# Four PSUM banks as single tiles and two as pairs, another order of the row pairs, and a 64-byte shift of the large SBUF pools

## The chip, the cores and the metric

The kernel runs on one NeuronCore of one Trainium2 chip. The metric is the device time of one execution in microseconds, as a median over runs. The engines named below are PE (TensorE, matmuls), PEld (its weight loads), DVE (VectorE), ACT (ScalarE), POOL (GpSimd) and SP (the queue from which weight loads are issued).

## The reference

A two-layer trunk on 256 tokens of width 2048, in float32. Each layer is a token mixer and then an MLP, with an RMS norm ahead of each and one at the end.

```
x (1, 256, 2048); D_FF = 8192
layer 0: x += conv_module(rms_norm(x))   # pw1 + GLU, causal depthwise conv of 31, LayerNorm, silu, pw2
         x += square(relu(rms_norm(x) @ mlp_w1[0])) @ mlp_w2[0]
layer 1: x += mla(rms_norm(x))           # w_in, low-rank q and kv, rotary key, 16 heads, softmax, w_o
         x += square(relu(rms_norm(x) @ mlp_w1[1])) @ mlp_w2[1]
out = rms_norm(x)
```

The four MLP products are the bulk: each is 256 x 2048 x 8192 or 256 x 8192 x 2048.

## The kernel before

**Split products.** A float32 operand is held as two parts, hi (rounded to the TensorE's fp32r) and lo (the rest). A product is three matmuls, hi·hi, lo·hi and hi·lo (`mm3`, L215 to L217). Weights come from DRAM as `raw` tiles by SP; ACT makes `hi` (L182 or L509), DVE makes `lo` (L186 or L510). Three `raw` tiles and six each of `hi` and `lo` are in turn. In `mm3` the activation (a 128x128 slice of a tile such as `gh`, `sh`, `fh`, `xh`, `xt`) is the operand that stands in the array and the weight tile, 512 columns wide, moves through it. In the plain up blocks (L796, L797) the weights stand and the activations, `xt`, move.

**The MLP.** It runs in two halves of 4096 hidden columns. The up product of a half has six steps in the order of `UP_PLAN`: four plain blocks of 512 columns each, and two up blocks (`up_block`), with two blocks of 512 columns together each. An up block takes the 2048 input rows as eight row pairs of 2 x 128 rows, in the order `UP_ORDER`. Four of them (2, 3, 4 and 5, `UP_MIXED`) are mixed: seven products (21 matmuls) stand for eight, of sums and differences of the input, prepared once (`fh`, `fl`), and of the weights, prepared per pair on DVE (`mixed_weights`: L517 to L519 change `raw`, L509 and L510 split the results). The other four are plain: eight products (24 matmuls) and only two `hi` and two `lo`. There are eight up blocks in a run, two for each layer and half. The down product of a half adds mixed and plain row pairs in the same way, for two column blocks at a time; the last one of the kernel ends with two single column blocks, and the last of these with a split end that the final norm follows. Their sums are in `Sums`: four banks `e`, in which row block t and column block c have one bank each, and four banks `u` for the mixed products.

**PSUM.** There are eight banks of 512 float32 values per partition. In the MLP the pool is four tiles of two banks each (`pair`); a single bank is half of such a tile (`acc_tile`, `spare`). A tile is given out again when its users are done, tile by tile, and both halves of a pair count as one tile.

**Order.** Each engine runs its instructions in the order in which the kernel writes them; instructions wait on semaphores for their inputs and for the buffer that they write.

**SBUF.** Tiles get their addresses in the order in which the pools are opened. A pad tile of `PAD_SMALL` columns (4 bytes each) stands ahead of the pools of each stage, so it shifts all of these.

Of the kernel before, what the change touches and what calls it, by code (L numbers as in the profile page):

```python
# [37 lines left out]
PAD_SMALL = 48  # L38
# [8 lines left out]
UP_PLAN, UP_ORDER, UP_MIXED = (4, 5, 0, 6, 2, 7), (0, 2, 3, 1, 4, 5, 6, 7), (2, 3, 4, 5)  # L47
# [35 lines left out]
def trunk_kernel(  # L83
# [33 lines left out]
    psum, psum_cx, spare = {}, [ExitStack()], []  # L117

    def repool(name, **banks):

        psum_cx[0].close()
        psum_cx[0] = ExitStack()
        psum.clear()
        spare.clear()
        for kind, n in banks.items():
            psum[kind] = psum_cx[0].enter_context(tc.tile_pool(name=kind + name, bufs=n, space=PSUM, reuse_waits="tile"))
# [147 lines left out]
    def to_T(src, k0, hi, lo, gain, rest=None):  # L274
# [12 lines left out]


        def lower():
            for j in range(2):  # L290
                lo_part(ps[j], hi(k0 + j), lo(k0 + j), gain[:, k0 + j : k0 + j + 1])

        if rest is None:
            lower()
        else:
            while rest:
                rest.pop(0)()
            rest.append(lower)
# [89 lines left out]
    def residual_stage(last, gain, r_scale=None, raw=None, by_steps=()):  # L388
# [18 lines left out]
        def prepare(n, only=None, half=None, out=None, rest=None):  # L407
            sl = columns(n, half)
            if last:
                if n in by_steps:  # L410
                    step()
                    steps.extend(turn_block(n, gain, raw))
                elif gain is not None:
                    while rest:
                        rest.pop(0)()
                    for j in range(2):
                        to_T(xs, 4 * n + 2 * j, xh, xl, gain, rest if j == 1 else None)
# [11 lines left out]
    def product_A(  # L429
        w, k_lo, nk, hi, lo, add, prepare, blocks=range(NNB), due=(), finish=None, before=None,  # L430
        units=None, banks=None, begun=None, beside=None, room=None,
# [12 lines left out]
        for n in blocks:  # L444
            ps = [acc_tile() for _ in range(T)] if banks is None else banks[n]
# [28 lines left out]
            if n_end:  # L474
                before()
                for t in range(T):
# [160 lines left out]
    def mlp(layer, ssq, next_gain, finish=None, before=None, beside=None, after_up=None):  # L637

        with ExitStack() as cx:
# [5 lines left out]
            repool(f"mlp{layer}", pair=4)  # L645
# [12 lines left out]
            def spread(r):  # L658
                o = [pair_tile() for _ in range(2)][0][:, 0, :]
# [56 lines left out]
            def up_block(hf, g, fs, copies):  # L716

                n = (hf * nkh + 4 * g) // 4
                sums = Sums(n, False, False)
# [18 lines left out]
                for t, z in enumerate(zs):  # L738
                    o = z.rearrange("p (c n) -> p c n", c=2)
                    nc.vector.tensor_tensor(o, sums.pe[t], o, op=ALU.add)  # L740
                    nc.scalar.activation(z, z, AF.Relu, scale=r_cols[0][:, t : t + 1])

                def turned():
                    pts = [a.rearrange("p b (k t n) -> p (b k) t n", t=T, n=P) for a in sums.pe]
# [11 lines left out]
                for _ in range(2):  # L756
                    pair_tile()
# [3 lines left out]
            for hf in range(HALVES):  # L761
# [10 lines left out]
                for nth, g in enumerate(UP_PLAN):  # L772
# [3 lines left out]
                    pairs = [pair_tile() for _ in range(2)]  # L776
                    ps = [a[:, b, :] for a in pairs for b in range(2)]
                    if layer > 0 and hf == nth == 0:
                        nc.vector.memset(ps[3][:, 0:1], 0.0)  # L779
# [30 lines left out]
                    for i, a in enumerate(pairs):  # L810
                        vi = v[:, 2 * i : 2 * i + 2, :]
# [78 lines left out]
    with ExitStack() as cx:  # L890
# [544 lines left out]
        product_A(conv_w_pw2[0], 0, KC, sh_kt, sl_kt, add, prepare, range(2, NNB), range(2))  # L1435
# [66 lines left out]
    with ExitStack() as cx:  # L1502
# [329 lines left out]
        with tc.manual_schedule():  # L1832
# [8 lines left out]
            free = [acc_tile() for _ in range(6)]  # L1841
            ps = [free[:2], free[2:4]]

            def kv_products(k, ts):
                u, j = divmod(k, 2)
                wh, wl = w_at(("kv", u), j)
                for t in ts:
                    for i in range(2):
                        ns = slice(i * NKV, (i + 1) * NKV)
                        if k == t == 0 and i == 1:  # L1850
                            for o in free[4:]:
                                nc.vector.memset(o[:, 0:1], 0.0)
                            for o in ps[1][::-1]:
                                nc.scalar.activation(o[:, 0:1], ident[:, 0:1], AF.Copy)
# [131 lines left out]
        product_A(mla_w_o[0], 0, H, oh_kt, ol_kt, add, prepare, range(2, NNB), range(2))  # L1986
# [90 lines left out]
```

## Time and profile before

| | |
|---|---|
| median of 3 runs | 1951.13 us (1950.62 to 1952.14) |
| profiled execution: its time, and the span of its trace | 1951.48 us, 1949.6 us |
| PE busy | 1928.1 us, 99% of the span |
| DVE busy | 1694.4 us, 87% |
| ACT busy | 1192.6 us, 61% |
| DMA | 193 GB/s on average |

Share of the chain of work that ended last: PE 86%, DVE 10%, ACT 2%. A busy PE does not say that nothing is lost: the ends of matmuls are modelled, and they overlap. Where PE loses time is seen from starts: from one start of a 128x512 matmul to the next it is about 0.23 us, and a larger step is a stall. The column in brackets behind a row of the timeline gives the idle time ahead of it and the instruction that ended it.

### The profile page before, as it was taken

How to read it: one execution, taken by the hardware profiler on the slowest of the kernel's cores; microseconds unless marked ns; L12 is line 12 of the kernel's file. 1: busy time of each engine (PE TensorE's matmuls, PEld its weight loads, DVE VectorE, ACT ScalarE, POOL GpSimd, SP SyncE). 2: the span in 40 equal slices, each digit the busy share in tenths (PEclk: the TensorE clock that was granted, in tenths of full speed). 3: DMA queues.
4: the chain of work that ended last, by engine and by line, in shares of the span. 5: the costliest groups of instructions: out<-in, count | busy, mean ns of one | idle time of the engine just before them, and what ended most of it. 6: DMA issues, size and time to landing. Idle time of an engine off the chain costs nothing.

```text
span 1949.6 us, 27537 instructions
## 1 busy us (share of the span) xinstructions
PE 1928.1 (99%) x10245; PEld 1654.1 (85%) x10245; DVE 1694.4 (87%) x2382; ACT 1192.6 (61%) x1655; POOL 248.7 (13%) x208
## 2 busy tenths in 40 slices
PE   9999999999999999999999999999999999999997
PEld 9999888888888888888889998888788888878886
DVE  7999988988989898899976766898999988898896
ACT  5667756656556656655576655566665556666554
POOL 6999200000010100000002310000000010000000
PEclk9999999999999999999999999999999999999998
DMA  7766455546575854655565545545647685565763
GB/s 227 213 187 182 160 186 191 200 154 212 194 243 187 248 196 163 216 190 199 195 195 151 141 152 173 178 167 195 225 149 238 219 242 180 195 216 195 226 206 119
DMA packets 214038, 375.43 MB, mean 193 GB/s; under 512 B 16392, under 2 KB 107792, under 8 KB 213648
## 3 DMA queue, kind: packets, MB, share of 16 engines
q1 hardware_dynamic: 208256, 363.28, 56.4%
q0 software_dynamic: 4320, 7.87, 2.3%
q10 hardware_dynamic: 1328, 2.52, 0.4%
q8 instruction: 80, 1.31, 0.3%
q14 instruction: 54, 0.44, 0.1%
HBM read 363.68 MB, written 2.10 MB: 188 GB/s over the span
## 4 chain that ended last, share of the span: by engine, by line
PE 86%; DVE 10%; ACT 2%; issue 2%; DMA 0%; DVEq 0%; ACTq 0%
PE pair L215 15%; PE pair L217 15%; PE pair L216 14%; PE pair L796 10%; PE acc L955 8%; PE pair L797 6%; PE acc L215 4%; PE acc L217 4%; PE acc L216 4%; PE acc L1419 2%; DVE lo L510 2%; DVE sum L1042 1%; DVE raw L517 1%; ACT hi L509 1%; DVE sl L538 1%
## 5 line engine op out<-in xcount | busy, mean ns | idle before, releaser
L182 ACT ACTIVATE hi<-raw 128x1024 fp32r<-128x1024 f32 (+2 forms) x510 | 508.1, 1029 | 182.9 <-DMA raw<-in_mlp_w 62.4
L186 DVE TENSOR_TENSOR lo<-raw,hi 128x1024 fp32r<-128x1024 f32 (+2 forms) x445 | 518.2, 1192 | 112.0 <-ACT hi L182 105.6
L509 ACT ACTIVATE hi<-raw 128x1024 fp32r<-128x1024 f32 x376 | 347.3, 948 | 320.5 <-DVE raw L517 191.8
L510 DVE TENSOR_TENSOR lo<-raw,hi 128x1024 fp32r<-128x1024 f32 x376 | 400.5, 1087 | 33.8 <-ACT hi L509 28.6
L796 PE MATMUL pair<-xt,hi 128*128 128x512 f32 x1024 | 357.2, 391 | 0.4 <-DVE pair L779 0.2
L797 PE MATMUL pair<-xt,lo 128*128 128x256 f32 x1024 | 288.6, 282 | 0.0
L796 PEld LDWEIGHTS pair<-xt,hi 128*128 128x128 f32 x1024 | 192.2, 188 | 41.2 <-issue 0.6
L215 PE MATMUL pair<-hi,gh 128*128 128x512 f32 (+1 forms) x516 | 203.5, 394 | 3.9 <-DVE xs L400 3.9
L217 PE MATMUL pair<-lo,gh 128*128 128x512 f32 (+1 forms) x516 | 202.4, 392 | 0.0
L216 PE MATMUL pair<-hi,gl 128*128 128x512 f32 (+1 forms) x516 | 200.7, 389 | 0.0
L797 PEld LDWEIGHTS pair<-xt,lo 128*128 128x128 f32 x1024 | 193.5, 189 | 0.5
L955 PE MATMUL acc<-xt,hi 128*128 128x256 f32 x1024 | 180.1, 281 | 0.4 <-ACT xt L1222 0.3
L215 PE MATMUL pair<-hi,sh 128*128 128x512 f32 x450 | 177.1, 393 | 0.0
L217 PE MATMUL pair<-lo,sh 128*128 128x512 f32 x450 | 176.5, 392 | 0.0
L216 PE MATMUL pair<-hi,sl 128*128 128x512 f32 x450 | 174.9, 389 | 0.0
L596 POOL DMA_DIRECT2D xs<-v x30 | 26.2, 909 | 1142.4 <-ACT v L614 1082.8
L1042 DVE SCALAR_TENSOR_TENSOR sum<-ub,w_dw,sum 128x256 f32<-128x256 f32 x409 | 164.4, 485 | 3.5 <-ACT sum L1012 3.0
L186 POOL TENSOR_TENSOR lo<-raw,hi 128x1024 fp32r<-128x1024 f32 x65 | 155.1, 2412 | 17.9 <-ACT hi L182 17.9
L955 PEld LDWEIGHTS acc<-xt,hi 128*128 128x128 f32 x1024 | 154.6, 188 | 1.2 <-ACT xt L1222 0.8
L955 PE MATMUL acc<-xt,lo 128*128 128x256 f32 x512 | 139.2, 279 | 0.0
L215 PEld LDWEIGHTS pair<-hi,gh 128*128 128x128 f32 x516 | 97.6, 189 | 24.1 <-ACT hi L182 3.8
L217 PEld LDWEIGHTS pair<-lo,gh 128*128 128x128 f32 x516 | 97.5, 189 | 22.1
(354 smaller groups left out, 3555.8 us busy)
## 6 DMA issues: line engine op xcount, KB each, us to landing
raw<-in_mlp_w SPq DMA_DIRECT2D x255, 1024.0 KB, 5.4
raw<-in_conv_w_pw SPq DMA_DIRECT2D x62, 512.0 KB, 5.1
raw<-in_conv_w_pw SPq DMA_DIRECT2D x16, 1024.0 KB, 5.0
raw<-in_mla_w_o SPq DMA_DIRECT2D x16, 1024.0 KB, 5.1
raw<-in_mla_w_kv_up SPq DMA_DIRECT2D x32, 256.0 KB, 3.8
xs<-v POOLq DMA_DIRECT2D x30, 256.0 KB, 7.7
raw<-in_mla_w_in SPq DMA_DIRECT2D x8, 576.0 KB, 3.8
raw<-in_mla_w_in SPq DMA_DIRECT2D x4, 1024.0 KB
```

The source lines that it names most:

```text
L182: nc.scalar.activation(hi, raw[:, js, :], AF.Copy)
L186: eng.tensor_tensor(lo, raw, hi.bitcast(F32), op=ALU.subtract)
L215: nc.tensor.matmul(ps, sh, mh, start=start, stop=False)
L216: nc.tensor.matmul(ps, sl, mh, start=False, stop=False)
L217: nc.tensor.matmul(ps, sh, ml, start=False, stop=stop)
L509: nc.scalar.activation(hi, src, AF.Copy)
L510: nc.vector.tensor_tensor(lo, src, hi.bitcast(F32), op=ALU.subtract)
L796: nc.tensor.matmul(ps[b], wh[:, bs], xhl(k), start=k == 0, stop=False)
L797: nc.tensor.matmul(ps[b][:, :S], wl[:, bs], xh(k), start=False, stop=k == KC - 1)
L955: nc.tensor.matmul(pss[c][b][:, :S], w[i][:, bs], (xh, xl)[j](k), start=k == i + j == 0, stop=end and k == k0 + nk - 1 and (i, j) == terms ...
L1042: nc.vector.scalar_tensor_tensor(out=out, in0=ubs[c][:, w : w + S], scalar=tap(c, w), in1=base, op0=ALU.mult, op1=ALU.add)
L1419: nc.tensor.matmul(ps2[b][t], x_kt(k, t), w[:, bs], start=k == g == i == 0, stop=k == KC - 1 and i == len(group) - 1,)
```

## The change

1. `UP_ORDER` becomes (0, 2, 1, 3, 6, 4, 5, 7): a plain pair stands between mixed pairs 2 and 3, and another between 3 and 4.
2. In the MLP the PSUM pool becomes four single banks (`acc`) and two pairs (`pair`), opened in one order in layer 0 and in the other in layer 1. `Sums` takes two pairs and four singles; in the down products the banks `e` are the pairs for the first two column blocks and the singles for the others. Plain up blocks after the first use four singles, and add up their halves in four operations of 256 columns rather than two of 512. The two halves at the very end of the kernel use two different pairs.
3. At the end of layer 0's MLP the eight transposes of a column block go to one pair and are issued together (`block_T`), with the `lo` parts of the last two of its four row blocks put off; before it was two tiles of one bank with four transposes each (`to_T`).
4. At three stage ends a bank is passed over by a memset of one column (`passed`, and `free[0]` in the attention stage), and two memsets and copies that did so before are left out.
5. `PAD_SMALL` goes from 48 to 64 columns: all pools behind it move by 64 bytes. For the large pools, whose tiles stand in the array, the offset of a tile goes from 64 to 0 modulo 128 bytes; `hi`, `lo`, `raw` (0), `xt` (32) and the pools on the right side stay where they were.

```
-PAD_SMALL = 48
+PAD_SMALL = 64
-UP_PLAN, UP_ORDER, UP_MIXED = (4, 5, 0, 6, 2, 7), (0, 2, 3, 1, 4, 5, 6, 7), (2, 3, 4, 5)
+UP_PLAN, UP_ORDER, UP_MIXED = (4, 5, 0, 6, 2, 7), (0, 2, 1, 3, 6, 4, 5, 7), (2, 3, 4, 5)
...
     def acc_tile():
-        if "pair" in psum:
-            if not spare:
-                both = pair_tile()
-                spare.extend(both[:, i, :] for i in range(2))
-            return spare.pop(0)
         return psum["acc"].tile([P, NB], F32, tag="acc", name=nm("acc"))
...
+    def block_T(src, k0, hi, lo, gain, rest):
+
+        ks = range(k0, k0 + NB // P)
+        ps = pair_tile().rearrange("p b (k n) -> p (b k) n", n=S)
+        for j, k in enumerate(ks):
+            for t in range(T):
+                nc.tensor.transpose(ps[:, j, t * P : (t + 1) * P], src[:, t, k * P : (k + 1) * P], ident)
+        for j, k in enumerate(ks):
+            hi_part(ps[:, j, :], hi(k), gain[:, k : k + 1])
+
+        def lower(js):
+            for j in js:
+                lo_part(ps[:, j, :], hi(ks[j]), lo(ks[j]), gain[:, ks[j] : ks[j] + 1])
+
+        while rest:
+            rest.pop(0)()
+        lower((0, 1))
+        rest.append(lambda: lower((2, 3)))
...
                 elif gain is not None:
-                    while rest:
-                        rest.pop(0)()
-                    for j in range(2):
-                        to_T(xs, 4 * n + 2 * j, xh, xl, gain, rest if j == 1 else None)
+                    if rest is None:
+                        for j in range(2):
+                            to_T(xs, 4 * n + 2 * j, xh, xl, gain)
+                    else:
+                        block_T(xs, 4 * n, xh, xl, gain, rest)
...
         for n in blocks:
+            for _ in range(passed if n == blocks[-1] else 0):
+                nc.vector.memset(acc_tile()[:, 0:1], 0.0)
             ps = [acc_tile() for _ in range(T)] if banks is None else banks[n]
...
                         for c in range(2):
-                            o = acc_tile()[:, :h]
+                            o = pair_tile()[:, 0, :h]
...
-        def __init__(self, n, by_dma, swap=None):
+        def __init__(self, n, by_dma, up=False):
             self.n, self.by_dma = n, by_dma
-            pairs = [pair_tile() for _ in range(4)]
-            self.pe, pu = (pairs[:2], pairs[2:])[:: -1 if (n > 0 if swap is None else swap) else 1]
-            self.e = [[a[:, c, :] for c in range(2)] for a in self.pe]
-            self.u = [a[:, c, :] for a in pu for c in range(2)]
+            self.pairs = [pair_tile() for _ in range(2)]
+            ps = [a[:, c, :] for a in self.pairs for c in range(2)], [acc_tile() for _ in range(4)]
+            e, self.u = ps[:: -1 if n > 0 and not up else 1]
+            self.e = [e[2 * t : 2 * t + 2] for t in range(T)]
...
-            repool(f"mlp{layer}", pair=4)
+            kinds = [("acc", 4), ("pair", 2)]
+            repool(f"mlp{layer}", **dict(kinds[:: -1 if layer else 1]))
...
-                    pairs = [pair_tile() for _ in range(2)]
-                    ps = [a[:, b, :] for a in pairs for b in range(2)]
-                    if layer > 0 and hf == nth == 0:
-                        nc.vector.memset(ps[3][:, 0:1], 0.0)
+                    if nth == 0:
+                        ends = [pair_tile() for _ in range(2)]
+                        ps = [a[:, b, :] for a in ends for b in range(2)]
+                    else:
+                        ps = [acc_tile() for _ in range(4)]
+                        ends = [a.rearrange("p (b n) -> p b n", b=1) for a in ps]
...
-        product_A(conv_w_pw2[0], 0, KC, sh_kt, sl_kt, add, prepare, range(2, NNB), range(2))
+        product_A(conv_w_pw2[0], 0, KC, sh_kt, sl_kt, add, prepare, range(2, NNB), range(2), passed=2)
...
-            free = [acc_tile() for _ in range(6)]
-            ps = [free[:2], free[2:4]]
+            free = [acc_tile() for _ in range(5)]
+            ps = [free[1:3], free[3:5]]
+            nc.vector.memset(free[0][:, 0:1], 0.0)
...
-        product_A(mla_w_o[0], 0, H, oh_kt, ol_kt, add, prepare, range(2, NNB), range(2))
+        product_A(mla_w_o[0], 0, H, oh_kt, ol_kt, add, prepare, range(2, NNB), range(2), passed=1)
```

How the order of the row pairs shows on DVE: the rows of one up block (the first of the run's) from the last weights of mixed pair 2 on. L510 (after the change L518) is the `lo` part of mixed weights, L517 to L519 (L525 to L527) their sums in `raw`, L186 (L180) the `lo` part of a plain pair. Before:

```order
686 L510 TENSOR_TENSOR lo_4835<-raw_4817,hi_4834 128x1024
687 L699 TENSOR_TENSOR gl_4769<-v_4770,gh_4768 128x1024
688 L510 TENSOR_TENSOR lo_4862<-raw_4859,hi_4861 128x1024
689 L510 TENSOR_TENSOR lo_4866<-raw_4859,hi_4865 128x512
690 L517 TENSOR_TENSOR raw_4859<-raw_4859 128x1024
691 L518 TENSOR_TENSOR raw_4859<-raw_4859 128x512
692 L519 TENSOR_TENSOR raw_4859<-raw_4859 128x512
693 L510 TENSOR_TENSOR lo_4873<-raw_4859,hi_4872 128x1024
694 L510 TENSOR_TENSOR lo_4877<-raw_4859,hi_4876 128x1024
695 L186 TENSOR_TENSOR lo_4904<-raw_4901,hi_4903 128x1024
696 L186 TENSOR_TENSOR lo_4908<-raw_4901,hi_4907 128x1024
697 L510 TENSOR_TENSOR lo_4938<-raw_4935,hi_4937 128x1024
```

And the same place after the change:

```order
692 L518 TENSOR_TENSOR lo_4855<-raw_4837,hi_4854 128x1024
693 L708 TENSOR_TENSOR gl_4783<-v_4784,gh_4782 128x1024
694 L180 TENSOR_TENSOR lo_4882<-raw_4879,hi_4881 128x1024
695 L180 TENSOR_TENSOR lo_4886<-raw_4879,hi_4885 128x1024
696 L518 TENSOR_TENSOR lo_4916<-raw_4913,hi_4915 128x1024
697 L518 TENSOR_TENSOR lo_4920<-raw_4913,hi_4919 128x512
698 L525 TENSOR_TENSOR raw_4913<-raw_4913 128x1024
699 L526 TENSOR_TENSOR raw_4913<-raw_4913 128x512
700 L527 TENSOR_TENSOR raw_4913<-raw_4913 128x512
701 L518 TENSOR_TENSOR lo_4927<-raw_4913,hi_4926 128x1024
702 L518 TENSOR_TENSOR lo_4931<-raw_4913,hi_4930 128x1024
703 L180 TENSOR_TENSOR lo_4958<-raw_4955,hi_4957 128x1024
```

The two rows of plain pair 1 now stand ahead of the seven of mixed pair 3 rather than behind them, and plain pair 6 stands behind pair 3.

The second place is on PE at the last column block of the kernel: the last matmuls of the block before it (`gh_16596`, `gh_16682`) and the first of the last one. A bracket names the engines on whose semaphores a matmul waits. Before:

```order
9536 L215 MATMUL pair_17233<-hi_17664,gh_16596 128x512
9537 L216 MATMUL pair_17233<-hi_17664,gl_16597 128x512
9538 L217 MATMUL pair_17233<-lo_17665,gh_16596 128x512
9539 L215 MATMUL pair_17232<-hi_17707,gh_15305 128x512 [waits DVE_49,Activation_49]
9540 L216 MATMUL pair_17232<-hi_17707,gl_15306 128x512
9541 L217 MATMUL pair_17232<-lo_17708,gh_15305 128x512
9542 L215 MATMUL pair_17233<-hi_17707,gh_15305 128x512 [waits DVE_49]
```

After the change:

```order
9532 L209 MATMUL acc_17326<-hi_17758,gh_16682 128x512
9533 L210 MATMUL acc_17326<-hi_17758,gl_16683 128x512
9534 L211 MATMUL acc_17326<-lo_17759,gh_16682 128x512
9535 L209 MATMUL acc_17325<-hi_17801,gh_15377 128x512 [waits Activation_49]
9536 L210 MATMUL acc_17325<-hi_17801,gl_15378 128x512
9537 L211 MATMUL acc_17325<-lo_17802,gh_15377 128x512 [waits DVE_49]
9538 L209 MATMUL acc_17327<-hi_17801,gh_15377 128x512
```

Before, the last column block goes on in the tiles 17232 and 17233 that hold the sums of the block before it in their other halves; after, it has tiles of its own, and the waits that are left in these rows are those for `hi` and `lo`.

More of the change, by code (lines that the diff above doesn't have):

```diff
@@ L272, in rms_rstd, with to_T @@
         return rsqrt(ms, T, EPS, name)
-    def to_T(src, k0, hi, lo, gain, rest=None):
+    def block_T(src, k0, hi, lo, gain, rest):
[13 more added lines that the diff above has]
+        rest.append(lambda: lower((2, 3)))
+    def to_T(src, k0, hi, lo, gain):
         pt = tr_tile()
@@ L286, in to_T @@
             hi_part(ps[j], hi(k0 + j), gain[:, k0 + j : k0 + j + 1])
-        def lower():
-            for j in range(2):
[L291 to L295, printed above, removed]
-            while rest:
-                rest.pop(0)()
-            rest.append(lower)
+        for j in range(2):
+            lo_part(ps[j], hi(k0 + j), lo(k0 + j), gain[:, k0 + j : k0 + j + 1])
     repool("c", acc=4, tr=1, sum=3)
@@ L430, in product_A @@
         w, k_lo, nk, hi, lo, add, prepare, blocks=range(NNB), due=(), finish=None, before=None,
-        units=None, banks=None, begun=None, beside=None, room=None,
+        units=None, banks=None, begun=None, beside=None, room=None, passed=0,
     ):
@@ L658, in spread @@
             def spread(r):
-                o = [pair_tile() for _ in range(2)][0][:, 0, :]
+                o = acc_tile()
                 for t in range(T):
@@ L739, in up_block @@
                     o = z.rearrange("p (c n) -> p c n", c=2)
-                    nc.vector.tensor_tensor(o, sums.pe[t], o, op=ALU.add)
+                    nc.vector.tensor_tensor(o, sums.pairs[t], o, op=ALU.add)
                     nc.scalar.activation(z, z, AF.Relu, scale=r_cols[0][:, t : t + 1])
                 def turned():
-                    pts = [a.rearrange("p b (k t n) -> p (b k) t n", t=T, n=P) for a in sums.pe]
+                    pts = [a.rearrange("p b (k t n) -> p (b k) t n", t=T, n=P) for a in sums.pairs]
                     for c in range(2):
@@ L809, in mlp @@
                     v = v_tile()
-                    for i, a in enumerate(pairs):
-                        vi = v[:, 2 * i : 2 * i + 2, :]
+                    nb = len(ps) // len(ends)
+                    for i, a in enumerate(ends):
+                        vi = v[:, nb * i : nb * (i + 1), :]
                         nc.scalar.activation(vi, a[:, :, S:], AF.Copy)
```

16 lines of the change are left out of this document (3 added, 13 removed).

## The prediction

> **What bounds the kernel now.** I read the busy times first, then the list of waits, then the timelines of PE, DVE and ACT around each wait.
>
> ```profile
> PE 1928.1 (99%) x10245; PEld 1654.1 (85%) x10245; DVE 1694.4 (87%) x2382; ACT 1192.6 (61%) x1655; POOL 248.7 (13%) x208
> ```
>
> PE is the bound: only 21.5 us of the span of 1949.6 are idle. An edit can give time in two ways alone: PE stops less, or its matmuls come closer together. The waits of PE that the edits touch:
>
> ```profile
> PE pair L215 <- ACT hi L509: 4.5, 9, 0.7
> PE pair L215 <- DVE xs L400: 3.9, 2, 3.4
> PE acc L215 <- DVE xt L228: 1.1, 1, 1.1
> PE pair L796 <- DVE pair L779: 0.2, 1, 0.2
> PE pair L796 <- DVE xs L400: 0.2, 1, 0.2
> ```
>
> Columns: us in total, times, the longest. These idle times understate the loss, since the ends of matmuls are modelled; what counts is the step from one start to the next, less the normal step. So I price each stall by starts.
>
> **The change part by part.**
>
> *1. The order of the row pairs.* PE in the first up block, and DVE and ACT beside it:
>
> ```profile
> 420.14 0.39 PE L217 MATMUL pair<-lo,fh 128*128 128x512 f32 x1
> ...
> 422.43 0.39 PE L215 MATMUL pair<-hi,fh 128*128 128x512 f32 x1
> ...
> 424.26 0.40 PE L217 MATMUL pair<-lo,fh 128*128 128x512 f32 x1
> 424.77 0.50 PE L215 MATMUL pair<-hi,fh 128*128 128x512 f32 x1
> 425.11 0.40 PE L216 MATMUL pair<-hi,fl 128*128 128x512 f32 x1
> 426.22 0.50 PE L215 MATMUL pair<-hi,fh 128*128 128x512 f32 x1 [0.71 <-ACT hi L509]
> ...
> 428.63 0.40 PE L215 MATMUL pair<-hi,xt 128*128 128x512 f32 x1
> ...
> 431.90 0.40 PE L217 MATMUL pair<-lo,xt 128*128 128x512 f32 x1
> ```
>
> ```profile
> 420.61 1.82 DVE L510 TENSOR_TENSOR lo<-raw,hi 128x1024 fp32r<-128x1024 f32 x2
> 422.35 1.22 DVE L517 TENSOR_TENSOR raw<-raw 128x1024 f32<-128x1024 f32 x1
> ...
> 424.93 2.49 DVE L510 TENSOR_TENSOR lo<-raw,hi 128x1024 fp32r<-128x1024 f32 x2
> 427.34 2.35 DVE L186 TENSOR_TENSOR lo<-raw,hi 128x1024 fp32r<-128x1024 f32 x2
> 429.61 1.82 DVE L510 TENSOR_TENSOR lo<-raw,hi 128x1024 fp32r<-128x1024 f32 x2
> ```
>
> ```profile
> 423.66 1.06 ACT L509 ACTIVATE hi<-raw 128x1024 fp32r<-128x1024 f32 x1 [2.95 <-DVE raw L517]
> 425.11 1.06 ACT L509 ACTIVATE hi<-raw 128x1024 fp32r<-128x1024 f32 x1 [0.39 <-DVE raw L519]
> ```
>
> From 420.14 to 422.43 are ten steps: 0.229 us each. A mixed pair takes PE 21 x 0.229 = 4.8 us, and DVE 427.34 - 420.61 = 6.7 us; a plain pair takes PE 24 steps, 5.5 us (5.6 with `xt`), and DVE 429.61 - 427.34 = 2.3 us. So each mixed pair puts DVE 1.9 us behind PE, and each plain pair lets it make up over 3. Before, mixed pairs 2 and 3 follow each other with DVE just ahead, and pair 3's sums of weights (L517, then ACT's L509 at 423.66 and 425.11) come late: the step 424.26 to 424.77 is 0.28 too long, that from 425.11 to 426.22 is 0.88. By starts, four up blocks show these two and 0.45 more before pair 5's `hi`, and one block shows 0.68: 4 x 1.61 + 0.68 = 7.1 us in 13 stalls.
>
> After, with PE and DVE as in this block up to DVE's 420.61 (pair 2's last `lo` and `gl`): plain pair 1 has its `lo` by 422.9, when PE begins it at 422.4 with the half that is done. Mixed pair 3's DVE work then ends 6.7 us later, at 429.6, with the first `hi` of its sums near 427; PE ends pair 1 at 428.0 and reaches those products near 430.1, 1.7 us or more after they are ready. Plain pair 6 takes PE from 432.9 to 438.5, DVE to 432.0. Pair 4 is done on DVE at 438.7 and pair 5 at 445.4, PE begins them at 438.5 and 443.3 and uses each one's last product's weights some 3.4 us later: 3.2 and 1.3 us of slack. Pair 7 has its `lo` at 446.6 and 447.8 for uses at 448.5 and 449.2. Tightest is pair 5, since 4 and 5 still stand next to each other. All 13 stalls go: **-6.9**, 0.2 kept for a late restart. Bounds: -7.1, and a return of some 0.6 per block if DVE comes 2 us later than here (below).
>
> The later plain up blocks add their halves in four DVE operations of 256 columns where there were two of 512, and copy likewise on ACT: by the row of a 128x256 addition in the tail below, 4 x 0.4 against 2 x 0.64, 0.3 us more on DVE in 12 blocks, and less for PE to wait on. It lies beside PE's 5.5 us of plain pair 0, which follows; without this cover it would be 12 x 0.3 = 3.6 us.
>
> *2. The PSUM tiles at the end.* PE at the last column block, then DVE and SP, then the second half-width product:
>
> ```profile
> 1909.69 0.40 PE L217 MATMUL pair<-lo,gh 128*128 128x512 f32 x1
> 1913.45 0.76 PE L215 MATMUL pair<-hi,gh 128*128 128x512 f32 x1 [3.37 <-DVE xs L400]
> ...
> 1918.71 0.52 PE L215 MATMUL pair<-hi,gh 128*128 128x512 f32 x1
> 1919.06 0.40 PE L216 MATMUL pair<-hi,gl 128*128 128x512 f32 x1
> ...
> 1939.37 0.28 PE L217 MATMUL pair<-lo,gh 128*128 128x256 f32 x1
> 1940.16 0.39 PE L215 MATMUL pair<-hi,gh 128*128 128x256 f32 x1 [0.52 <-DVE xs L400]
> ```
>
> ```profile
> 1907.29 1.22 DVE L186 TENSOR_TENSOR lo<-raw,hi 128x1024 fp32r<-128x1024 f32 x1
> ...
> 1912.62 1.28 DVE L400 TENSOR_TENSOR xs<-pair,xs 128x512 f32<-128x512 f32 x2
> 1913.82 2.95 DVE L186 TENSOR_TENSOR lo<-raw,hi 128x512 fp32r<-128x512 f32 x3
> ...
> 1939.68 0.42 DVE L400 TENSOR_TENSOR xs<-pair,xs 128x256 f32<-128x256 f32 x1 [0.72 <-PE pair L217]
> ```
>
> ```profile
> 1902.80 12.11 SPq L172 DMA_DIRECT2D raw<-in_mlp_w  x4
> ```
>
> PE stops for 1913.45 - 1909.69 - 0.23 = 3.53 us until the additions of the block before have left the other half of the same pair. Then twelve steps take 1918.71 - 1913.45 = 5.26 us where 12 x 0.229 = 2.75 are normal, and the thirteenth 0.12 too long: 2.63 us at a lower clock. The step at 1939.37 is 0.79 where 0.12 is normal: 0.67. Together 6.83. After, the sums have banks of their own; the order of PE shows `hi` and `lo` as the only waits left, and these are there (`lo` by 1908.5). PE goes on at 1909.92, without the stop and the slow steps. What comes due next are the last weights. PE needs units 0 and 1 until 1918.15 and unit 4 from 1923.65 (24 + 12 + 24 matmuls later). Unit 4's DMA waits for unit 1's `raw`, freed at about 1914.5 as DVE goes through the x3 at 1913.82, and the last of the four issues from 1902.80 ends at 1914.91. With some 5.3 us to land, 1.0 for each `hi` and 1.2 for each `lo`, the halves are there at 1922.6 and 1923.7, 1.1 to 1.4 us before their use. **-6.7.** Bounds: -6.8, and -5 if that DMA is 2 or 3 us slower.
>
> [...]
>
> *3. `block_T` at MLA's start.* DVE there:
>
> ```profile
> 986.19 1.66 DVE L228 SCALAR_TENSOR_TENSOR xt<-pair,vecs,xt 128x256 fp32r<-128x256 f32 x4 [0.80 <-ACT xt L221]
> 987.76 1.28 DVE L629 TENSOR_TENSOR xs<-pair,xs 128x512 f32<-128x512 f32 x2
> ```
>
> The wait of 1.1 has DVE's chain of `lo` parts (0.4 each) and additions (0.6 each) behind it, which keeps its length: the put-off parts move behind the additions, so that the first attention product can start some 0.6 us earlier, and the transposes after it wait for the same last `lo`, at about 992. **+0.2**, between -0.6 (the earlier start is kept) and +0.6 (ACT's four more `hi` in a row come late).
>
> *4. Banks at the stage ends.* PE at the second of the two places:
>
> ```profile
> 1249.02 0.40 PE L796 MATMUL pair<-xt,hi 128*128 128x512 f32 x1
> 1249.25 0.28 PE L797 MATMUL pair<-xt,lo 128*128 128x256 f32 x1
> 1249.75 0.50 PE L796 MATMUL pair<-xt,hi 128*128 128x512 f32 x1 [0.22 <-DVE pair L779]
> ```
>
> The step from 1249.25 is 0.50 for 0.12: 0.38. The other 0.2 of the list, at 301, is 0.35 by starts. The MLP's first block then gets banks that were free earlier; the memsets that the change adds wait only for DVE's own earlier additions, with nothing of PE's queued behind them. **-0.6**; between 0 and -0.7.
>
> *5. The 64-byte shift.* No trace shows these tiles at 0 modulo 128. What I have: with `fh` in the array (64 modulo 128) a step is 0.229 us. With `xt` (32 modulo 128), 428.63 to 431.90 are fourteen steps of 0.2336. In plain up blocks the standing weights lie at 0 modulo 128, and the step is again 0.23 (1249.02 to 1249.25; 228.5 ns as a mean over 1,012 of them). So 0 is nearer to 64 than to 32. The matmuls that are touched, for the most part:
>
> ```profile
> L215 PE MATMUL pair<-hi,gh 128*128 128x512 f32 x508 | 201.1, 396 | 3.4 <-DVE xs L400 3.4
> ...
> L215 PE MATMUL pair<-hi,sh 128*128 128x512 f32 x450 | 177.1, 393 | 0.0
> ...
> L215 PE MATMUL pair<-hi,fh 128*128 128x512 f32 x224 | 89.2, 398 | 5.0 <-ACT hi L509 4.5
> ```
>
> Three forms of each: 3 x (508 + 450 + 224) = 3,546. At 0.5 ns less each this is -1.8 us; at `xt`'s 4.6 ns more, +16.3. I take **-1.0**.
>
> [...]
>
> Sum: -6.9 - 6.7 + 0.2 - 0.6 - 1.0 = -15.0. The profiled execution took 1951.48 us, 0.35 above the median of the runs shown: 1951.1 - 15.0 = **1936**.
>
> **The rivals.**
>
> *A. The debt of DVE comes back at pairs 4 and 5.* They still stand together, and 1.3 us of slack is little on an engine busy 87%. For it: the 1.9 us per mixed pair. Against it: pair 6 lets DVE make up 3. If it waits 0.6 in each of the eight blocks, 1936 + 4.8 = **1941**.
>
> *B. The last weights replace the banks.* The 5 us of a DMA are what the tail's slack is made of. If unit 4 comes 2 to 3 us late, PE stops there, short of the slow clock: **1939**.
>
> *C. The wait at 1909.69 has another cause,* and the banks do not remove it: the additions came last, but something else close behind them holds PE as long. Then parts 1, 4 and 5 alone are left: 1951.1 - 8.3 = **1943**. Against it: `lo` of the first unit is done by 1908.5, 5 us before PE starts.
>
> *D, on the other side: the shift slows the matmuls.* If a standing tile at 0 modulo 128 costs what `xt`'s does at 32, every matmul with `gh`, `sh`, `fh` in the array takes 4.6 ns more: 1936 + 1.0 + 16.3 = **1953**, and up to 1959 with the smaller groups of that kind. It decides from about 4 ns on. Against it: the plain blocks' weights at 0.
>
> **How the numbers follow.** My forecast 0.52, A 0.13, B 0.10, C 0.08, D 0.08, and 0.09 for what I do not see, a third of it a larger gain (the shift giving more than 0.5 ns per matmul). The range reaches from 1931, under all terms at their best (1934) by 3 for the shift, to 1945, above C: 0.52 + 0.13 + 0.10 + 0.08 and a little of the rest. Within 0.2% (3.9 us, about what a measurement of this kernel can tell from no change) lies little: 0.05 of the unseen. Faster 0.86; slower 0.09, D's and 0.01 of the unseen.
>
> **What would show it.** Part 1: no row of PE's waits on `hi` of the mixed weights; wrong if the up blocks show steps over 0.4 us at pair 5. Part 2: no PEclk below full before the final norm, the step at the last column block 0.23; wrong if a wait for `lo` or `raw` stands there. Part 3: transposes again near the same distance from the last down product. Part 4: no wait of L805 (L796 before). Part 5: steps with `gh` or `fh` of 0.229 or a little less, or 0.2336. The forecast as a whole is wrong if PE's idle time falls by less than 8 us, or if the steps lengthen.

## The result and the profile after

The changed kernel takes 1928.19 us (median, 1927.75 to 1929.88) against 1950.88 before: a ratio of 0.9887, 95% interval 0.9870 to 0.9904, so 22.7 us faster. The forecast was 1936 with a range from 1931 to 1945. The sign held, the size did not: the gain was 1.5 times the one forecast, and the time lies under the range. The profiled execution took 1929.88 us with a span of 1928.1; the span of before was 1949.6.

The page's row of busy times, then PE's longest waits after the change (us in total, times, longest):

```profile
PE 1910.2 (99%) x10245; PEld 1651.3 (86%) x10245; DVE 1695.5 (88%) x2407; ACT 1190.2 (62%) x1677; POOL 249.0 (13%) x208
```

```profile
PE acc L805 <- DVE v L615: 3.6, 6, 1.1
PE acc L209 <- DVE xt L222: 1.6, 1, 1.6
PE acc L1143 <- POOL ident masks.py:199: 1.6, 1, 1.6
PE tr L292 <- DVE acc L1853: 0.9, 1, 0.9
```

The waits for the mixed `hi` (4.5) and for the additions at the tail (3.9) are gone, and so are those for L779 and at 301. But PE's idle time fell only from 21.5 to 17.9 us, and it has a new first entry: L805, the plain up block that follows an up block, waits 3.6 us in six places for L615, the last of the additions that empty the banks of the mixed products. These stalls vary: the profiled execution is the longest of the four, and in a kernel with the same up blocks (`e8_two_halves`, below) they are 2.8 us by starts where they are 4.6 here. PE's busy time fell by 17.9 us with the same 10,245 matmuls. So most of the gain does not stand in a list of waits at all. Where it is, 24 rows of plain pair 7 show, the first and the last of them here, before and after (PE's timeline):

```profile
445.80 0.39 PE L215 MATMUL pair<-hi,xh 128*128 128x512 f32 x1
...
451.06 0.39 PE L217 MATMUL pair<-lo,xh 128*128 128x512 f32 x1
```

```profile
445.80 0.39 PE L209 MATMUL pair<-hi,xh 128*128 128x512 f32 x1
...
451.01 0.39 PE L211 MATMUL pair<-lo,xh 128*128 128x512 f32 x1
...
452.18 0.28 PE L806 MATMUL acc<-xt,lo 128*128 128x256 f32 x1
453.10 0.50 PE L805 MATMUL acc<-xt,hi 128*128 128x512 f32 x1 [0.64 <-DVE v L615]
```

Before, 23 steps from start to start take 5.26 us, 228.7 ns each; after, 5.21 us, 226.5 ns. Over all undisturbed steps (up to 260 ns) with a tile of the large pools in the array the mean is 229.05 ns before (4,796 steps) and 226.82 after (4,844): 2.23 x 4,850 = 10.8 us. The last two rows are one of the new waits: a step of 0.92 us where 0.12 is normal.

The tail is as forecast: PE's timeline passes from one column block to the last (`acc` 17325 starts at 1895.46) without a stop, and the slow steps are gone (granted clock 1.00 from 1895 to 1915).

```profile
1895.23 0.39 PE L211 MATMUL acc<-lo,gh 128*128 128x512 f32 x1
1895.46 0.39 PE L209 MATMUL acc<-hi,gh 128*128 128x512 f32 x1
1895.69 0.39 PE L210 MATMUL acc<-hi,gl 128*128 128x512 f32 x1
```

The start of the attention became worse. PE's timeline there:

```profile
980.77 0.39 PE L211 MATMUL acc<-lo,gh 128*128 128x512 f32 x1
982.79 0.38 PE L209 MATMUL acc<-hi,xt 128*128 128x288 f32 x1 [1.63 <-DVE xt L222]
...
984.32 0.29 PE L211 MATMUL acc<-lo,xt 128*128 128x288 f32 x1
985.56 1.06 PE L292 MATMUL tr<-ident,xs 128*128 128x128 f32 x8 [0.94 <-DVE acc L1853]
```

By starts these two stalls are 1.79 and 1.10 us, 2.9 together, against 1.6 before.

The account of the span by starts: steps -10.8, stalls on the mixed `hi` -7.1, new stalls on L615 +4.6 (0.46 to 1.24 us each), tail -6.8, stage ends -0.7, attention +1.3: -19.5 of the 21.5 us. The other 2.0 are spread, for the most part over stalls under 0.2 us; the steps of 256 columns give 0.5 of them.

### The profile page after: what moved, and what is told of

The parts are those of the page before. It is cut to its first block, busy times and chain, and to the rows that moved or that the text cites. A ratio compares the mean times of both kernels' runs of the same rounds, so it can differ in the third digit from the quotient of the medians.

```text
span 1928.1 us, 27561 instructions
## 1 busy us (share of the span) xinstructions
PE 1910.2 (99%) x10245; PEld 1651.3 (86%) x10245; DVE 1695.5 (88%) x2407; ACT 1190.2 (62%) x1677; POOL 249.0 (13%) x208
## 4 chain that ended last, share of the span: by engine, by line
PE 88%; DVE 7%; ACT 2%; DMA 2%; issue 2%; ACTq 0%; DVEq 0%
PE acc L211 10%; PE acc L209 10%; PE acc L210 10%; PE acc L805 9%; PE pair L209 8%; PE pair L210 8%; PE pair L211 8%; PE acc L965 8%; PE acc L806 5%; PE pair L805 3%; PE acc L1429 2%; PE pair L806 2%; DVE lo L180 1%; DVE lo L518 1%; DVE sum L1052 1%
## 5 line engine op out<-in xcount | busy, mean ns | idle before, releaser
L180 DVE TENSOR_TENSOR lo<-raw,hi 128x1024 fp32r<-128x1024 f32 (+2 forms) x445 | 518.1, 1191 | 96.2 <-ACT hi L176 88.9
L517 ACT ACTIVATE hi<-raw 128x1024 fp32r<-128x1024 f32 x376 | 346.9, 948 | 316.1 <-DVE raw L525 187.4
L518 DVE TENSOR_TENSOR lo<-raw,hi 128x1024 fp32r<-128x1024 f32 x376 | 399.8, 1086 | 26.8 <-ACT hi L517 20.8
L805 PE MATMUL acc<-xt,hi 128*128 128x512 f32 x768 | 269.0, 392 | 3.6 <-DVE v L615 3.6
L806 PE MATMUL acc<-xt,lo 128*128 128x256 f32 x768 | 216.4, 282 | 0.0
L805 PEld LDWEIGHTS acc<-xt,hi 128*128 128x128 f32 x768 | 144.1, 188 | 35.7 <-DVE v L615 5.8
L180 POOL TENSOR_TENSOR lo<-raw,hi 128x1024 fp32r<-128x1024 f32 x65 | 155.1, 2411 | 17.5 <-ACT hi L176 17.5
L965 PEld LDWEIGHTS acc<-xt,hi 128*128 128x128 f32 x1024 | 154.6, 188 | 1.1 <-ACT xt L1232 0.6
L806 PEld LDWEIGHTS acc<-xt,lo 128*128 128x128 f32 x768 | 145.1, 189 | 0.3
L965 PE MATMUL acc<-xt,lo 128*128 128x256 f32 x512 | 139.2, 279 | 0.0
L525 DVE TENSOR_TENSOR raw<-raw 128x1024 f32<-128x1024 f32 x94 | 114.5, 1219 | 0.4
L209 PE MATMUL acc<-hi,sh 128*128 128x512 f32 x289 | 112.6, 390 | 0.0
L211 PE MATMUL acc<-lo,sh 128*128 128x512 f32 x289 | 112.5, 389 | 0.0
L210 PE MATMUL pair<-hi,gl 128*128 128x512 f32 (+1 forms) x264 | 101.9, 386 | 0.0
L211 PE MATMUL pair<-lo,gh 128*128 128x512 f32 (+1 forms) x264 | 101.9, 386 | 0.0
L209 PE MATMUL pair<-hi,gh 128*128 128x512 f32 (+1 forms) x264 | 101.9, 386 | 0.0
```

Source lines behind the costliest of these rows:

```text
L180: eng.tensor_tensor(lo, raw, hi.bitcast(F32), op=ALU.subtract)
L209: nc.tensor.matmul(ps, sh, mh, start=start, stop=False)
L210: nc.tensor.matmul(ps, sl, mh, start=False, stop=False)
L211: nc.tensor.matmul(ps, sh, ml, start=False, stop=stop)
L517: nc.scalar.activation(hi, src, AF.Copy)
L518: nc.vector.tensor_tensor(lo, src, hi.bitcast(F32), op=ALU.subtract)
```

## The experiments

**Each part by itself.** Theory S held that the shorter steps come from the 64-byte shift; its rival was that they come from the new PSUM banks. Theory D held that the wait on L615 is DVE's debt from the mixed pairs; its rival, that the new banks bring it.

The shift alone:

```
-PAD_SMALL = 48
+PAD_SMALL = 64
```

> The kernel before with the 64-byte shift alone (PAD_SMALL 64). Theory S: the shorter step of the 128x512 matmuls after the change (226.8 ns where gh, sh, fh, xh stand in the array, against 229.0 to 229.6 before) comes from the shift, about 4,900 matmuls x 2.3 ns: 1951 - 11 = 1940 us, with the waits of before kept (mixed hi 4.5 us, tail 3.9 us). Rival B: the steps shortened because the sums lie in other PSUM banks; then the steps stay at 229 and the time at 1951.

Measured: 1945.43 us (1943.55 to 1947.18) against 1950.03, ratio 0.9975 (0.9964 to 0.9986), so -4.6 us. The steps are 226.97 ns on 4,793: the shift shortens the matmuls, with no other bank or order changed, and rival B falls. But less than half of the 10.8 us arrived. PE's waits of this kernel:

```profile
PE pair L215 <- ACT hi L509: 5.9, 14, 0.7
PE pair L215 <- ACT hi L182: 3.9, 1, 3.9
...
PE acc L215 <- DVE xt L228: 1.1, 1, 1.1
PE pair L217 <- DVE lo L510: 1.0, 3, 0.5
PE pair L279 <- DVE xt L228: 1.0, 1, 1.0
```

All of PE's stalls over 0.2 us add up, by starts, to some 22.5 us here and 16.8 before. A faster PE reaches DVE's and ACT's results earlier and waits for them: 14 times rather than 9 for the mixed `hi`, and at the last column block for `hi` of the next weights (3.9) rather than for the additions (3.4). After that stop three steps are normal, and the eight that follow take 0.43 us each, 3.4 us in all (granted clock 0.83 from 1905 to 1915).

The order of the row pairs alone:

```
-UP_ORDER = (0, 2, 3, 1, 4, 5, 6, 7)
+UP_ORDER = (0, 2, 1, 3, 6, 4, 5, 7)
```

> The kernel before with the new order of the row pairs alone. Theory D: the 7.1 us of stalls on mixed hi go, and the DVE debt of pairs 4 and 5 comes back in the next plain block, which waits for the additions that empty the mixed banks: some 4 us, so 1951 - 7.1 + 4.0 = 1948 us. Rival: that wait belongs to the new banks; then the order alone gives the full 7.1: 1944 us and no wait on L607.

Measured: 1943.43 us, ratio 0.9963 (0.9950 to 0.9976), -6.6. Its waits, and its tail in PE's timeline:

```profile
PE pair L215 <- DVE xs L400: 3.9, 2, 3.4
PE pair L796 <- DVE v L607: 1.6, 5, 0.5
```

```profile
1903.65 0.40 PE L217 MATMUL pair<-lo,gh 128*128 128x512 f32 x1
1907.43 0.47 PE L215 MATMUL pair<-hi,gh 128*128 128x512 f32 x1 [3.38 <-DVE xs L400]
1907.73 0.40 PE L216 MATMUL pair<-hi,gl 128*128 128x512 f32 x1
...
1910.54 0.40 PE L216 MATMUL pair<-hi,gl 128*128 128x512 f32 x1
```

The wait after the up blocks (here on L607, the same addition) is there with the old banks, so it belongs to the order, as theory D has it, but it is small: 2.7 us by starts, not 4. The gain of 6.6 lies between the theory's 3 and the rival's 7, next to the latter. A part of it may be the clock's, as the second block shows: after the same stop of 3.38 us one step is 0.30 and the next are 0.234, with a granted clock of 1.00 from 1905 to 1915. Before, after 3.37 us, they were 0.43 for twelve matmuls, with 0.50 granted from 1913.45 to 1918.71. So the clock granted after this stop differs between executions. How much of it the medians hold is open; the granted clock was 0.997 in 5 of the 31 executions of the kernel before that these experiments were compared with, 0.998 in 23 and 0.999 in 3, and 0.997 in the profiled one.

The banks, the transposes and the passed banks alone (the changed kernel without the new order and without the shift):

```
-PAD_SMALL = 64
+PAD_SMALL = 48
-UP_ORDER = (0, 2, 1, 3, 6, 4, 5, 7)
+UP_ORDER = (0, 2, 3, 1, 4, 5, 6, 7)
```

> The changed kernel with the old order of row pairs and without the shift: banks, block_T and passed banks alone. Theory D: tail 6.8 and stage ends 0.7 gained, 1.3 lost at the start of the attention: 1951 - 6.2 = 1945 us, no new wait after the up blocks, mixed hi waits kept at 4.5. Rival (the wait after the up blocks belongs to the banks): 3.6 us of waits on L615 here too, 1949 us.

Measured: 1942.80 us, ratio 0.9959 (0.9945 to 0.9974), -7.2. There is no wait on L615. PE's waits:

```profile
PE acc L209 <- ACT hi L517: 2.0, 8, 0.3
...
PE pair L209 <- ACT hi L517: 1.0, 4, 0.3
PE tr L292 <- DVE acc L1853: 0.9, 1, 0.9
...
PE acc L209 <- DVE xt L222: 0.4, 1, 0.4
```

The gain is 1 us larger than theory D had it. Two differences are seen: the loss at the attention (0.9 + 0.4 of waits, about as before) is not there without the shift, and the stalls of the mixed pairs over 0.15 us are 6.3 us by starts where they were 7.1.

Everything but the shift:

```
-PAD_SMALL = 64
+PAD_SMALL = 48
```

> The changed kernel without the shift (PAD_SMALL 48). Theory S: steps back at 229, the waits after the up blocks a little smaller since DVE has more time: 1928 + 10 to 11 = 1938 to 1939 us. Rival B: steps stay at 226.8, time at 1928.

Measured: 1935.74 us, ratio 0.9923 (0.9906 to 0.9939), -14.3. The steps are at 228.94 ns again, and the waits are small:

```profile
PE tr L292 <- DVE acc L1853: 0.9, 1, 0.9
PE acc L805 <- DVE v L615: 0.7, 3, 0.3
...
PE acc L209 <- DVE xt L222: 0.4, 1, 0.4
```

So the shift is worth 0.9923 - 0.9887 = 0.36%, 7.0 us, in the changed kernel, less than the 10 to 11 expected. The wait on L615 grows from 0.7 to 3.6 with it (1.6 to 4.6 by starts), the two at the attention from 1.3 to 2.5: 10.8 - 3.0 - 1.3 = 6.5, near these 7.0 us.

**What the shift changes.** Theory R: the distance between the standing and the moving tile counts, modulo 128 bytes. Rival A: the place of the standing tile alone. Two kernels put the weights (`hi`, `lo`, `raw`) at 64, once with the large pools at 64 too, once with them at 0.

```
-PAD_CONST = 8
+PAD_CONST = 24
```

> The changed kernel with all tiles of the left side another 64 bytes on: hi, lo and raw at 64 modulo 128, and gh, sh, fh, xh at 64 too. Theory R: what counts is the distance of the standing tile from the moving one, modulo 128; it is 0 as in the changed kernel, so the steps stay at 226.8 ns and the time at 1928 us. Rival A: what counts is the place of the standing tile alone; then the steps are 229 with the pattern 226, 229, 232 as before, and the time is about 1936 us.

```
-PAD_CONST = 8
-PAD_SMALL = 64
+PAD_CONST = 24
+PAD_SMALL = 48
```

> The changed kernel with hi, lo and raw at 64 modulo 128 and gh, sh, fh, xh at 0. Theory R (distance): 64 apart as in the kernel before, so 229 ns with the pattern 226, 229, 232, about 1936 us. Rival A (standing tile alone): 226.8 ns, 1928 us.

Measured: with both at 64 the steps of the large pools' tiles are 226.88 ns, with the weights at 64 and the tiles at 0 they are 228.93. Rival A falls: standing at 64 was fast (226.88 ns) with the moving tile at 64, and standing at 0 was slow (228.93) with it at 64. The times, of one execution each, missed the expectation all the same: 1937.59 and 1945.06 us. The shift of the weights also moved them against `xt`: in the plain up blocks, where weights stand and `xt` moves, the steps went from 228.62 to 232.15 and 233.59 ns, 3.6 and 5.1 us in all, and the steps of 256 columns took 2.2 and 3.1 us more. The two values differ although the weights stand at 64 and `xt` moves at 32 in both kernels; so the places of the two tiles do not settle the step of these blocks, and no run shows what else does.

That made the place of `xt` the next question. Three kernels moved the right side, where `xt` lies, from 32 to 0, to 96 and to 64 modulo 128 (the last one on top of the new queue order, below).

```
-PAD_RIGHT = 48
+PAD_RIGHT = 56
```

> The changed kernel with the tiles of the right side 32 bytes lower: xt, kTh, qTh, vv at 0 modulo 128 like the weights. Theory R: the 273 steps with xt standing go from 233.2 to 226.8 ns, the 1,007 of the plain up blocks (xt moving) from 228.6 to 226.8, the 190 of 288 columns by some 6 ns: -1.7 - 1.8 - 1.1 = -4.6, of which a third may come back as waits for DVE: 1924 to 1926 us. Rival A (standing tile alone): the plain up blocks do not change, 1926 us or less gain.

```
-PAD_RIGHT = 48
+PAD_RIGHT = 64
```

> The changed kernel with the right side (xt) at 96 modulo 128 instead of 32. In the products with xt standing the distance to the weights is then 32 the other way round; theory R, the distance counts either way: 233 as now. In the plain up blocks, where the weights stand and xt moves, distance 0 gave 234.8 ns, 32 gave 228.6; there no rule is at hand; if only the amount of the distance counts it is 228.6 again and the time 1928 us, if its sign counts it is near the 232 that standing at 64 and moving at 32 gave, 1928 + 4 = 1932 us.

```
-PAD_RIGHT = 48
+PAD_RIGHT = 40
```

> The kernel with the new queue order on DVE (1924.1 us) and the right side (xt) at 64 modulo 128. Theory R (distance): the 273 steps with xt standing go from 233.2 to about 229, -1.1 us. In the plain up blocks (xt moving, weights standing at 0) the distances seen so far gave 234.8 (0), 232.5 (32 one way) and 228.5 (32 the other way); 64 lies between the last two on the circle, so 229 to 231 and +0.5 to +2.5 us: 1923.5 to 1925.5. If 64 is the best one there, 226.8 and -1.8 - 1.1: 1921.

Measured: 1937.28 us (ratio 0.9935, 0.9919 to 0.9952), 1934.22 us (one execution), and 1927.66 us (0.9887, 0.9869 to 0.9904; the same without the move is 1924.06). All three are slower, and none reached what was expected of it; theory R fails in the plain up blocks. The means of the steps of 512 columns, by the place of the tile that stands and of the one that moves, modulo 128 bytes, over all undisturbed steps of one profiled execution:

| what stands, what moves | stands at | moves at | ns | steps |
|---|---|---|---|---|
| large pools, weights | 0 | 0 | 226.82 | 4,844 |
| large pools, weights | 64 | 64 | 226.88 | 4,846 |
| large pools, weights | 64 | 0 | 229.05 | 4,796 |
| large pools, weights | 0 | 64 | 228.93 | 4,846 |
| xt, weights | 0 | 0 | 227.8 | 273 |
| xt, weights | 32 | 0 | 233.2 | 273 |
| xt, weights | 64 | 0 | 233.3 | 273 |
| xt, weights | 96 | 0 | 233.2 | 273 |
| weights, xt (plain up blocks) | 0 | 32 | 228.62 | 1,007 |
| weights, xt | 0 | 0 | 234.78 | 1,007 |
| weights, xt | 0 | 64 | 231.42 | 1,014 |
| weights, xt | 0 | 96 | 232.46 | 1,006 |
| weights, xt | 64 | 32 | 232.15 | 1,007 |
| weights, xt | 64 | 32 | 233.59 | 1,009 |

For the split products (`mm3`) the step was shortest at equal places, with the large pools standing (226.82 and 226.88 ns) and with `xt` (227.8). For other distances no one rule fits: 64 apart cost 2 ns with the large pools and 6 with `xt`. In the plain up blocks, where a matmul of 512 columns alternates with one of 256, equal places (0 and 0) gave the longest 512-column step, 234.78 ns; the 256-column step after it was then 1.9 ns shorter (116.5 for 118.4). What the addresses do inside the chip no run shows. The 32 at which `xt` lay is the best of its four places for the time of the kernel, since what the plain up blocks would lose outweighs the 273 steps.

**The new wait after the up blocks.** DVE's timeline of the changed kernel at the first one:

```profile
447.36 0.68 DVE L612 TENSOR_TENSOR v<-acc,v 128x512 f32<-128x512 f32 x1
447.96 1.21 DVE L180 TENSOR_TENSOR lo<-raw,hi 128x1024 fp32r<-128x1024 f32 x1
449.09 0.68 DVE L613 TENSOR_TENSOR v<-acc,v 128x512 f32<-128x512 f32 x1
450.62 1.22 DVE L180 TENSOR_TENSOR lo<-raw,hi 128x1024 fp32r<-128x1024 f32 x1 [0.84 <-ACT hi L176]
451.76 0.68 DVE L614 TENSOR_TENSOR v<-acc,v 128x512 f32<-128x512 f32 x1
452.36 0.68 DVE L615 TENSOR_TENSOR v<-acc,v 128x512 f32<-128x512 f32 x1
```

In the code the additions L612 to L615 are written ahead of the next weights. On DVE two `lo` of the following block stand between them: outside the two regions that the kernel orders by hand (`manual_schedule`), the framework's scheduler sets the order of an engine's instructions, so that the sentence above on order, that each engine runs in the order in which the kernel writes, does not hold here. The second of these `lo` belongs to weights that land late:

```profile
449.53 2.01 ACT L176 ACTIVATE hi<-raw 128x1024 fp32r<-128x1024 f32 x2 [2.77 <-DMA raw<-in_mlp_w]
```

ACT waits for them and makes their `hi`, so DVE idles 0.84 us and works 1.1 on the `lo` with L614 and L615 queued behind, while PE needs the banks they free. Theory Q: this place in the queue makes the wait. Rival: DVE is behind with its work in any order. The experiment queues that unit's `lo` behind L615:

```
-            nc.vector.tensor_tensor(b, u5, b, op=ALU.add)
+            self.parts_end = nc.vector.tensor_tensor(b, u5, b, op=ALU.add)
...
                         sums.parts(*(z[:, c * NB : (c + 1) * NB] for z in zs for c in range(2)))
+                        parts_end.append(sums.parts_end.ins)
...
-            r_cols, late = [], []
+            r_cols, late, parts_end = [], [], []
...
-                        wj = load_split([rows(mlp_w1[layer], 4 * u, 4, c0, NB)], 4)
+                        with tc.issue_after(parts_end.pop()) if u == 1 and parts_end else ExitStack():
+                            wj = load_split([rows(mlp_w1[layer], 4 * u, 4, c0, NB)], 4)
```

> The changed kernel with the lo parts of the second weight unit of the plain block after an up block queued on DVE behind the additions that empty the mixed banks (L612 to L615). Theory Q: the new wait on L615 (3.6 us, 4.6 by starts) comes from DVE's queue, in which a lo that waits for its DMA and ACT stands ahead of the last two additions; then the wait goes, 1928 - 4 = 1924 us. Rival D: DVE is simply behind with its work; then the time stays within 1 us, the wait moves to lo.

Measured: 1924.06 us (1923.15 to 1925.59), ratio 0.9868 (0.9854 to 0.9883) to the kernel before: 4.1 us less than the changed kernel, as theory Q has it. A second pair of kernels, with other transposes (`e8_two_halves` and `e10_parts_first_two_halves`, below), repeats it: 1927.59 without the new queue order and 1924.02 with it. DVE's timeline and PE's waits:

```profile
447.29 1.21 DVE L180 TENSOR_TENSOR lo<-raw,hi 128x1024 fp32r<-128x1024 f32 x1
448.43 0.68 DVE L613 TENSOR_TENSOR v<-acc,v 128x512 f32<-128x512 f32 x1
449.14 0.69 DVE L614 TENSOR_TENSOR v<-acc,v 128x512 f32<-128x512 f32 x1
449.75 0.68 DVE L615 TENSOR_TENSOR v<-acc,v 128x512 f32<-128x512 f32 x1
450.35 1.22 DVE L180 TENSOR_TENSOR lo<-raw,hi 128x1024 fp32r<-128x1024 f32 x1
```

```profile
PE acc L209 <- DVE xt L222: 1.1, 1, 1.1
PE tr L292 <- DVE acc L1855: 0.9, 1, 0.9
```

L615 ends at 450.4 rather than 453.0, and no wait on it is left; it did not turn into a wait for `lo`.

The same kernel without the shift tells what the shift is worth when this wait cannot take it back:

```
-PAD_SMALL = 64
+PAD_SMALL = 48
```

> The kernel with the new queue order on DVE, without the 64-byte shift. Theory G: the shift takes 2.3 ns off about 4,900 matmuls, 11 us, and gave 4 to 6 of these back as waits for DVE; where the queue order takes these waits away it is worth at least 9.5: 1924.1 + 9.5 = 1933.6 us or more. Rival: the shift is worth the 7.5 us that it was in the changed kernel, wherever it is: 1931.5.

Measured: 1933.39 us, ratio 0.9914 (0.9900 to 0.9929), so the shift is worth 9.3 us here, 7.0 in the changed kernel and 4.6 in the kernel before. Theory G wanted 9.5 or more and its rival 7.5; the measured 9.3 (9.0 from the ratios) lies nearer to G, a little under its bound.

**The start of the attention.** Theory M: the grouping of the transposes (`block_T`) makes it late. Its rival: PE is earlier, and DVE and ACT take as long as before. The experiment makes them in two groups of four again, each in one bank of a pair, first with the changed kernel, then with the new queue order.

```
-        ps = pair_tile().rearrange("p b (k n) -> p (b k) n", n=S)
+        for half in range(2):
+            ks = (k0 + 2 * half, k0 + 2 * half + 1)
+            pt = pair_tile()[:, 0, :]
...
+            if half == 0:
+                lower()
+            else:
+                rest.append(lower)
```

> The changed kernel with the transposes of a column block at the end of layer 0 in two groups of four again (one bank of a pair each), hi and lo of the first group ahead of the second, as in the kernel before. Theory M: it is the grouping of the eight transposes (ACT makes eight hi in a row, then DVE six lo) that makes the attention start late, 1.6 + 0.9 us of waits against 1.1 + 0.2; then 1928 - 1.3 = 1927 us. Rival: PE just comes there earlier, DVE and ACT take as long as before; then the waits and the time stay within 0.5 us.

> The queue order on DVE (additions of the mixed banks ahead of the second weight unit) together with the transposes in two groups. Theory M: 1924 - 1.3 = 1922.8 us; rival: 1924.

Measured: 1927.59 us (1926.86 to 1928.46) against the changed kernel's 1928.19, and 1924.02 (1922.97 to 1925.32) against 1924.06; both differences lie inside the spread of the executions. The two stalls add up by starts to 1.16 + 1.51 = 2.7 us in the first, 2.9 with `block_T`. The rival holds; theory M falls. The shift alone on the kernel before, with its old transposes, has 1.18 + 1.30 + 0.31 = 2.8 us there, and the changed kernel without the shift 0.54 + 1.09 = 1.6.

The fastest kernels measured are those with the new queue order, with either grouping of the transposes: 1924.06 and 1924.02 us, 0.9868 of the time before.

## Why the prediction was right or wrong

**Part 1, the order: right, with a return in another place than its rival had it.** -6.9 was forecast. By itself the order gave -6.6, and 1942.80 - 1935.74 = 7.1 on top of the banks. All 13 stalls on mixed `hi` went. Rival A had priced the debt of DVE at 4.8 us and put it at pairs 4 and 5. The changed kernel has 4.6 us of new stalls, not there but behind pair 7, at the additions that free the banks; I had followed DVE's ledger to pair 7's `lo` and stopped. They are not the debt itself: with the additions ahead in DVE's queue they go. Without the shift they are only 1.6.

**Parts 2 to 4: right in sum.** -6.7 + 0.2 - 0.6 = -7.1 was forecast, and these parts alone gave -7.2. Rival B did not come: unit 4's last `lo` ends at 1909.5, and PE runs through. That a stop of 2 to 3 us would have been short of the slow clock was my estimate, and no run shows it; in the trace of before the granted clock was 1.00 from 1910.0 to 1912.1 and 0.50 from 1912.2, some 2 us into the stop. The 2.63 us of slow clock in the tail's term (granted clock 0.50 from 1913.45 to 1918.71) were that execution's: the kernel with the new order alone has the same stop and hardly a slow step, and the one with the shift alone a stop of 3.9 us and eight slow steps. That the sum of these parts came out within 0.1 us is in part luck.

**Part 5, the shift: wrong, and the step that failed.** I took -1.0, from the plain up blocks' 228.5 ns with standing weights at 0. It gave -7.0 in the changed kernel and 10.8 by steps. Those blocks were the wrong neighbour: there `xt` moves at 32, and the runs show that what stands and what moves must be seen together. The row for the case in question, both at the same place, was not in the trace of before, and I bounded a gain by half a nanosecond because one other stream had it. The bound of the loss (+16.3) was far wider than that of the gain (-1.8) with no better reason. The terms without this one make -14.0 us, and the changed kernel without the shift measured -14.3. With the sum at 1937 before it, and -7.0 for -1.0, the forecast would have been 1930. Rival D, longer steps, did not come. A larger gain from the shift had been given a third of 0.09.

The step of the same matmul was 226.8 or 229 ns by the place of one tile relative to the other; where in the chip the 2 ns arise no run shows.

**Part 3's place.** The 1.3 us lost at the attention are not `block_T`'s. They are the shift's: with it the two stalls are 2.7 to 2.9 us under either grouping (2.1 to 2.4 with the new queue order), without it 1.6. PE is done with its own part sooner, and the chain of DVE and ACT work that it then needs is not shortened; this reading is argued from the stalls alone. This was not in my sum, since I priced the shift as a gain that the other engines let through whole.

**The prediction's own signs.** It called the whole forecast wrong if PE's idle time fell by less than 8 us. It fell by 3.6: the waits for the mixed `hi` and the tail's additions (8.4) went, but 3.6 came on L615 and 1.2 more at the attention. It also wanted no wait of L805. The one at the stage end went, and L805 is where the new waits stand.

## What to carry to other kernels

Where one engine is 99% busy, look at the step between its instructions, not only at its waits: 2.23 ns on 4,850 matmuls were the largest term here, and no list of waits shows them. When such a step shortens, follow the other engines for as many microseconds as it gives: of 10.8 us, between 4.6 and 9.3 arrived, by how far DVE and ACT were ahead of PE. Bound an unknown cost below as widely as above, and take a neighbour for it only where all operands are alike.

## What the runs showed of the hardware

The step of a split 128x512 fp32r product depended on the places of both its tiles in SBUF: 226.8 ns where standing and moving tile had equal addresses modulo 128 bytes (227.8 with `xt` standing), 229 at 64 apart with the large pools standing (in steps of 226, 229 and 232 by turns), 233 with `xt` standing at 32, 64 or 96 and the weights moving at 0. In a stream that alternates 512 and 256 moving columns the equal place (0 and 0) had the longest 512-column step, 234.8 against 228.6, and there the places were not all that counted: one and the same pair of places gave 232.15 and 233.59. And the same stop of 3.37 to 3.38 us was followed by twelve steps of 0.43 us in one execution (granted clock 0.50) and by one of 0.30 and then steps of 0.234 in another (1.00); a stop of 3.9 us was followed by three normal steps and then eight of 0.43.
